# Two of five paired steps moved one place earlier, and three weight sums batched together

## The chip, the cores and the metric

The kernel runs on one core of one Trainium2 chip. The metric is the device time of one execution in microseconds. The program has one launch; its inputs are laid out on the host beforehand, by moving blocks only.

## The reference

One layer over 512 tokens of width 1024, in float32:

```python
h = rms_norm(x, norm_mix_g)
cb, cc, cin, q, k, v, f_logit, g_logit = jnp.split(h @ w_in, split_idx, axis=-1)
y_conv = (cb * causal_dwconv(cc * cin, conv_mix_w)) @ w_out_conv
y_attn = forgetting_attention(q, k, v, log_sigmoid(f_logit + b_f)) @ w_out_attn
g_conv, g_attn = jnp.split(sigmoid(g_logit + b_gate), 2, axis=-1)
x = x + (g_conv * y_conv + g_attn * y_attn) @ w_o
h = rms_norm(x, norm_ffn_g)
a, b = jnp.split(causal_dwconv(h @ w_up, conv_ffn_w), 2, axis=-1)   # 2 x 2816 wide
x = x + (silu(a) * b) @ w_down
return rms_norm(x, norm_f_g)
```

The change touches the last product pair: the up projection (1024 to 2 x 2816), its three-tap convolution along the sequence, and, by what it moves, the down projection.

## The kernel before

Activations lie transposed, channels on the 128 partitions and the 512 tokens along the free dimension. Every product is made of three float32r products: each operand is split into a high half (a copy, rounded) and a low half (the difference), and high x high, low x high and high x low are added in PSUM. For a weight tile the scalar engine makes the high half (`wh_...`, L279) and VectorE the low half (`wl_...`, L283) from what a DMA brought (`raw_...`, L221, issued by SyncE). There are five buffers for raw tiles and two each for the halves, so a split waits for TensorE to be done with the tile two before.

**Steps.** The hidden width is worked through in 22 steps `j` of 128 hidden channels, each with a tile of `a` and one of `b`. Steps 0 to 11 are the first half, then come 12 "down steps" that use what is there; steps 12 to 21 are the second half, followed by the remaining down steps and a plain remainder. A *plain* step is two blocks (`up{2j}`, `up{2j+1}`), each a full product over 8 blocks of the width, 48 matmuls of 128x256 (`p_up`). A block first runs 8 matmuls with the high half of the weight and then needs the low half. A *pair* (steps in `UPS`) multiplies its two tiles at once, as a two by two block product with seven instead of eight multiplications (Strassen's scheme in Winograd's form). Its weights come in four tiles, P, F, P, F (768, 1024, 768, 1024 columns), in which P holds plain blocks and F holds sums of blocks; its products (`us`) go to four PSUM banks and are combined by VectorE. Of each P the first 12 matmuls use the high half. The function `up_pair` does this, `pair` issues the products and asks for the splits.

**After the products** VectorE multiplies by the row scale (L1125, L1127: the evacuation, in place in PSUM for steps up to the last pair, and into the SBUF tile `xg` after it), `taps` makes the convolution (scalar engine L615, VectorE L616 and L619), and `glu` applies silu (L1147) and has GpSimd multiply (L1150 `ge` for an even step, L1157 `go` for an odd one). Two steps 2q and 2q+1 make one hidden pair `q`; with the odd one, `glu` puts off the sums of the hidden pair (L1167 to L1172) and their split into halves (scalar engine L1176, VectorE L1177, `gh`, `gl`). They are set free by the second, third and fourth weight split after that and stand between later splits. In the second half the taps and the `glu` of a pair are held back until the first block of the next step:

```python
z = p if j <= UPS[-1] else fz(f"fz{j}{s_}")
...
if j in UPS and ph:
    held_up.append(lambda: glu(ph, j, [tapped(j, s_, z) for s_, z in enumerate(uu)]))
```

With the last pair, once its products are done, the tile that held the summed inputs is used anew as `xg`: x1 is loaded into it (L1109, issued by GpSimd), and the scalar engine splits a part of it (L1358).

**Weight sums.** The F tiles are sums of weight blocks, which DMAs alone make in DRAM (`sum`): SyncE copies (L140) and GpSimd issues adding DMAs (L143), six operations for each group of two tiles, one at a time from a list (`tick`) as weights are split. `MIXED` says how many groups of the list take turns with each other: operation one of all of the batch, then operation two, and so on. Groups 14, 15 and 16 (`sum14` to `sum16`) belong to the three pairs of the second half, 17 to 19 to the down steps.

**Order.** On TensorE, GpSimd's DMAs and SyncE the order is that in which the program is written. On the scalar engine and VectorE a scheduler sets the order at build time, and each engine then runs its own in order. In the names of instructions a number after `up` is the tile (step 20 has `up40` and `up41`), and P36 to P41 are the P tiles of the three pairs.

Of the kernel before, what the change touches and what calls it, by code (L numbers as in the profile page):

```python
# [52 lines left out]
)  # L53
GS = 2
NFF = len(STEPS[0]) + len(STEPS[1])
UPS = (3, 7, 12, 15, 18)
NUP = NFF + 2 * (8 - GS)
MIXED = (4, 2, 4, 4, 2, 4, 2)

PLAIN = [(m, k) for m in (6, 7) for k in range(*PHASES[1])]  # L60
PCUTS = (0, 4, 12, 20)
# [3 lines left out]
def block_kernel(ctx, tc, xT, vecs, wv, win, wmix, wo, wup, wst, wdp, outT):  # L65
# [56 lines left out]
    for (j0, j1), n0, n1 in zip(PHASES, (0, len(STEPS[0])), (len(STEPS[0]), NFF - 1)):  # L122
        groups += [[NUP + 2 * i, NUP + 2 * i + 1] for i, j in enumerate(UPS) if j0 <= j < j1]
        groups += [list(range(n, min(n + 2, n1))) for n in range(n0, n1, 2)]
    groups.append([NFF - 1])
    nstep = [len(d) for d in STEPS[0] + STEPS[1]] + [2] * (2 * (KB - GS) + 2 * len(UPS))
    todo = []
# [26 lines left out]
    i0 = 0  # L154
    for n in MIXED:
        todo += [op for ops in zip(*map(group, range(i0, i0 + n))) for op in ops]
# [11 lines left out]
    def up_n(j):  # L168
        return [NUP + 2 * UPS.index(j) + d for d in range(2)]

# [14 lines left out]
    for ph, (j0, j1) in enumerate(PHASES):  # L185
        for j in range(j0, j1):
            if j in UPS:
                for m in up_n(j):
# [899 lines left out]
    def up_pair(j):  # L1088

        nonlocal xg, x1  # L1090
        flush([("xf", q) for q in range(4)])
        p23, p45, p16, p7 = banks = [acc(f"us{j}{i}") for i in range(4)]
        pair(up_n(j), x1_form, banks)
        z = fp.tile([P, S], F32, tag="fu", name=f"uz{j}", bufs=3)
        u = fp.tile([P, S], F32, tag="fu", name=f"uu{j}", bufs=3)[:, : S // 2]
        lo, hi = halves
        with after_split():
            nc.scalar.activation(z[:, lo], p16[:, lo], AF.Copy)
            nc.vector.tensor_add(z[:, hi], p16[:, hi], z[:, lo])
            nc.vector.tensor_add(u, p7[:, lo], z[:, hi])  # L1100
            nc.vector.tensor_add(z[:, hi], p45[:, hi], z[:, hi])
            nc.vector.tensor_add(p23, p23, z)
            p45h = p45.rearrange(halves_of, h=2)
            nc.vector.tensor_add(p45h, p45h, u.unsqueeze(1).to_broadcast([P, 2, S // 2]))
        if j == UPS[-1]:
            xg = xfp.tile([P, 4 * KB, 2 * P], F32, tag="xf", name="xg")
            x1 = xg[:, : 2 * KB].rearrange(whole, h=2)
            for a in range(0, KB, 4):
                nc.gpsimd.dma_start(x1[:, a : a + 4, :], x1d[:, a : a + 4, :])  # L1109
        return p23, p45  # L1110

    def up(ph, j, rb2, pu=None):
        uu = []
        if j in UPS:
            pu = up_pair(j)
# [416 lines left out]
```

## Time and profile before

| | |
|---|---|
| time, median of 3 runs | 690.75 us (690.72 to 690.81) |
| profiled execution | 690.7 us, span 688.9 us |
| granted TensorE clock, mean | 0.998 |
| TensorE busy | 680.0 us (99%) |
| VectorE busy | 547.3 us (79%) |
| scalar engine busy | 364.6 us (53%) |
| GpSimd busy | 184.2 us (27%) |
| second half's up steps, by TensorE's rows | 523.6 to 629.6 us |

A row of the timeline gives start, length, engine, line, operation, output<-inputs, and, in brackets, how long the engine had been idle and who ended that. Rows of one operation that follow each other are merged (x2). Matmuls overlap, so their pace is read from start to start, not from their lengths. PE is TensorE, DVE VectorE, ACT the scalar engine, POOL GpSimd, SPq the queue of SyncE.

### The profile page before, as it was taken

What the parts mean: (1) busy time and instruction counts of PE and PEld (TensorE: products, weight loads), DVE (VectorE), ACT (ScalarE), POOL (GpSimd) and SP (SyncE); (2) the same over time, 40 slices, a digit from 0 to 9 for tenths busy, and PEclk for the clock granted to TensorE, in tenths of its full rate; (3) what the DMA queues carried; (4) which work ended last, traced back from release to release, by engine and by line L of the source; (5) the groups of instructions that cost most, each with busy time, mean ns of one, the idle gap of its engine ahead of it and who ended that gap; (6) DMA issues with size and microseconds to landing.
All of it is one profiled execution on the core that took longest, in us unless ns stands there. A gap on an engine that the chain in (4) does not pass through costs nothing.

```text
span 688.9 us, 14690 instructions
## 1 busy us (share of the span) xinstructions
PE 680.0 (99%) x5916; PEld 677.8 (98%) x5916; DVE 547.3 (79%) x864; ACT 364.6 (53%) x581; POOL 184.2 (27%) x209
## 2 busy tenths in 40 slices
PE   9999999999999999999999999999999999999996
PEld 8999999999999999999999999999999999999996
DVE  6677777886687877768987989987665889999885
ACT  6575556554564544446654635545444445456563
POOL 5123745444021010233502141330131322222000
PEclk9999999999999999999999999999999999999999
DMA  8626957478579797888985859679799987674623
GB/s 295 208 89 217 198 154 174 100 184 167 131 221 279 214 262 197 240 270 281 213 225 133 227 119 293 156 216 253 219 290 309 251 193 183 187 239 132 188 78 123
DMA packets 66117, 139.64 MB, mean 203 GB/s; under 512 B 5856, under 2 KB 30432, under 8 KB 65792
## 3 DMA queue, kind: packets, MB, share of 16 engines
q1 hardware_dynamic: 44592, 105.72, 46.7%
q0 software_dynamic: 20736, 32.28, 26.9%
q8 instruction: 46, 0.75, 0.4%
q10 hardware_dynamic: 720, 0.69, 0.3%
q14 instruction: 23, 0.19, 0.1%
HBM read 132.32 MB, written 49.81 MB: 264 GB/s over the span
## 4 chain that ended last, share of the span: by engine, by line
PE 89%; DVE 6%; ACT 2%; issue 2%; DMA 1%; ACTq 0%; POOL 0%; SPq 0%; DVEq 0%; POOLq 0%
PE p_up L312 18%; PE p_in L312 14%; PE dn L330 13%; PE gs L330 8%; PE p_wo L312 6%; PE us L330 6%; PE p_up L330 6%; PE yc L330 3%; PE ya L312 3%; PE o L705 2%; PE pa L524 2%; PE pb L526 1%; PE tp L690 1%; PE pdB L312 1%; PE pdA L312 1%
## 5 line engine op out<-in xcount | busy, mean ns | idle before, releaser
L143 POOL DMA_DIRECT2D sum<-in_wst_dram x66 | 70.8, 1163 | 122.3 <-DMA sum<-sum 93.0
L312 PE MATMUL p_in<-xf,wh_in 128*128 128x256 f32 x576 | 95.7, 278 | 0.0
L312 PE MATMUL p_up<-x1h,wh_up 128*128 128x256 f32 x416 | 81.1, 276 | 0.0
L312 PEld LDWEIGHTS p_in<-xf,wh_in 128*128 128x128 f32 x576 | 80.4, 188 | 0.7
L312 PE MATMUL p_up<-x1l,wh_up 128*128 128x256 f32 x416 | 81.0, 276 | 0.0
L312 PE MATMUL p_up<-x1h,wl_up 128*128 128x256 f32 x416 | 80.9, 276 | 0.0
L279 ACT ACTIVATE wh_F<-raw_F 128x1024 fp32r<-128x1024 f32 (+1 forms) x42 | 44.2, 1052 | 66.7 <-PE dn L330 26.2
L283 DVE TENSOR_TENSOR wl_F<-raw_F,wh_F 128x1024 fp32r<-128x1024 f32 (+1 forms) x42 | 53.4, 1272 | 28.8 <-ACT wh_F L279 28.5
L312 PEld LDWEIGHTS p_up<-x1h,wh_up 128*128 128x128 f32 x416 | 62.7, 188 | 0.0
L312 PEld LDWEIGHTS p_up<-x1l,wh_up 128*128 128x128 f32 x416 | 62.6, 188 | 0.0
L312 PEld LDWEIGHTS p_up<-x1h,wl_up 128*128 128x128 f32 x416 | 62.5, 188 | 0.0
L312 PE MATMUL p_in<-xf,wl_in 128*128 128x256 f32 x288 | 56.6, 278 | 0.1
L279 ACT ACTIVATE wh_up<-raw_up 128x1024 fp32r<-128x1024 f32 x34 | 36.0, 1057 | 38.2 <-PE p_up L312 27.9
L279 ACT ACTIVATE wh_P<-raw_P 128x768 fp32r<-128x768 f32 (+1 forms) x42 | 35.1, 836 | 36.4 <-PE dn L330 15.9
L283 DVE TENSOR_TENSOR wl_P<-raw_P,wh_P 128x768 fp32r<-128x768 f32 (+1 forms) x42 | 40.2, 956 | 12.5 <-ACT wh_P L279 6.8
L283 DVE TENSOR_TENSOR wl_up<-raw_up,wh_up 128x1024 fp32r<-128x1024 f32 x34 | 42.3, 1246 | 7.6 <-ACT wh_up L279 7.6
L312 PEld LDWEIGHTS p_in<-xf,wl_in 128*128 128x128 f32 x288 | 43.5, 188 | 0.3 <-DVE wl_in L283 0.3
L1150 POOL TENSOR_TENSOR ge<-fu,fu 128x512 f32<-128x512 f32 x11 | 20.2, 1832 | 67.5 <-DVE fu L619 34.0
L330 PE MATMUL dn<-gh,wh_F 128*128 128x256 f32 x156 | 36.4, 276 | 0.0
L330 PE MATMUL dn<-gl,wh_F 128*128 128x256 f32 x156 | 36.3, 276 | 0.0
L283 DVE TENSOR_TENSOR wl_in<-raw_in,wh_in 128x1024 fp32r<-128x1024 f32 x24 | 30.2, 1258 | 6.1 <-ACT wh_in L279 6.0
L279 ACT ACTIVATE wh_in<-raw_in 128x1024 fp32r<-128x1024 f32 x24 | 25.3, 1056 | 10.8 <-issue 3.4
(361 smaller groups left out, 2106.0 us busy)
## 6 DMA issues: line engine op xcount, KB each, us to landing
raw_F<-sum SPq DMA_DIRECT2D x41, 512.0 KB, 5.4
raw_up<-in_wup_dram SPq DMA_DIRECT2D x34, 512.0 KB, 5.9
raw_P<-in_wst_dram SPq DMA_DIRECT2D x41, 384.0 KB, 4.8
raw_in<-in_win_dram SPq DMA_DIRECT2D x24, 512.0 KB, 3.6
sum<-in_wst_dram POOLq DMA_DIRECT2D x41, 256.0 KB, 6.3
sum<-in_wst_dram SPq DMA_DIRECT2D x20, 512.0 KB, 8.7
sum<-in_wst_dram POOLq DMA_DIRECT2D x20, 512.0 KB, 9.6
sum<-sum SPq DMA_DIRECT2D x40, 256.0 KB, 5.7
```

The costliest lines, as they stand in the source:

```text
L143: return lambda: keep(nc.gpsimd.dma_start(dst, src, accum_op=ALU.add))
L279: ins = nc.scalar.activation(hi, raw, AF.Copy)
L283: ins = nc.vector.tensor_sub(lo, raw, hi.bitcast(F32))
L312: keep(nc.tensor.matmul(out[:, cs], w, x[:, cs], start=start and i == 0 and c == 0, stop=stop and i == 2 and c == len(cut) - 1,))
L330: keep(nc.tensor.matmul(out, wl if x == 1 else wh, xl if x == 2 else xh, start=opens and bk not in seen, stop=closes and bk not in left,))
L524: keep(nc.tensor.matmul(pa[t][:, :VW], xt, w[:, :VW], start=start, stop=stop))
L526: keep(nc.tensor.matmul(pb[t], xt, w[:, VW:], start=start and t % 2 == 0, stop=stop and t % 2 == 1))
L690: keep(nc.tensor.transpose(tp[:, ks], pt[:, ks], ident))
L705: keep(nc.tensor.matmul(o[:, os_], vv[:, kb, pr, e, :], x[:, kb, cs], start=e == 0 and kb == 0 and i == 0, stop=e == 1 and kb == nk - 1 an ...
L1150: keep(nc.gpsimd.tensor_mul(ge, a.rearrange(halves_of, h=2), b.rearrange(halves_of, h=2)))
```

## The change

The second half's pairs are steps 12, 14 and 17 in place of 12, 15 and 18. The groups of weight sums stay the same in number; those of the three pairs now take turns in one batch of three, and those of the first three groups of down steps in another, in place of a batch of two and one of four. The last pair is one step earlier, and with it the load of x1 and the point from which evacuations go to `xg`.

```diff
-UPS = (3, 7, 12, 15, 18)
+UPS = (3, 7, 12, 14, 17)
 NUP = NFF + 2 * (8 - GS)
-MIXED = (4, 2, 4, 4, 2, 4, 2)
+MIXED = (4, 2, 4, 4, 3, 3, 2)
```

On VectorE, before, ahead of the first weight split of pair 18 (`go7`, `ge7`: sums of steps 14 and 15; `fu161`, `fu170`: taps of steps 16 and 17):

```order
L1167 TENSOR_TENSOR go7_7524<-ge7_7304 128x256
L619 SCALAR_TENSOR_TENSOR fu161_7581<-p_up33_7531,vec_64,fu161_7581 128x510
L1127 TENSOR_TENSOR p_up34_7588<-p_up34_7588,rb_n2_4660 128x512
L1168 TENSOR_TENSOR go7_7524<-go7_7524,ge7_7304 128x256
L1171 SCALAR_TENSOR_TENSOR go7_7524<-go7_7524 128x256
L1177 TENSOR_TENSOR gl_4720<-ge7_7304,gh_4719 128x2x256
L616 SCALAR_TENSOR_TENSOR fu170_7638<-p_up34_7588,vec_64,fu170_7638 128x511
L1172 SCALAR_TENSOR_TENSOR go7_7524<-go7_7524 128x256
L619 SCALAR_TENSOR_TENSOR fu170_7638<-p_up34_7588,vec_64,fu170_7638 128x510
L1177 TENSOR_TENSOR gl_4720<-go7_7524,gh_4719 128x512 x3
L283 TENSOR_TENSOR wl_P40_7725<-raw_P40_7420,wh_P40_7724 128x768
```

On the same engine in the changed program, ahead of the first weight split of step 20, two steps behind pair 17 (`go8`, `ge8`: sums of steps 16 and 17; `fu181`, `fu190`: taps of steps 18 and 19):

```order
L1167 TENSOR_TENSOR go8_7800<-ge8_7577 128x256
L619 SCALAR_TENSOR_TENSOR fu181_7857<-xg_7713,vec_64,fu181_7857 128x510
L1168 TENSOR_TENSOR go8_7800<-go8_7800,ge8_7577 128x256
L1127 TENSOR_TENSOR xg_7713<-p_up38_7864,rb_n2_4660 128x512
L1171 SCALAR_TENSOR_TENSOR go8_7800<-go8_7800 128x256
L1177 TENSOR_TENSOR gl_4720<-ge8_7577,gh_4719 128x2x256
L1172 SCALAR_TENSOR_TENSOR go8_7800<-go8_7800 128x256
L616 SCALAR_TENSOR_TENSOR fu190_7914<-xg_7713,vec_64,fu190_7914 128x511
L1177 TENSOR_TENSOR gl_4720<-go8_7800,gh_4719 128x512
L619 SCALAR_TENSOR_TENSOR fu190_7914<-xg_7713,vec_64,fu190_7914 128x510
L1177 TENSOR_TENSOR gl_4720<-go8_7800,gh_4719 128x512 x2
L283 TENSOR_TENSOR wl_up40_7999<-raw_up40_7693,wh_up40_7998 128x1024
```

The same operations stand ahead of a split in both; the split is now that of an up tile, the taps read `xg` in place of PSUM, and L1168 comes ahead of the evacuation.

On the scalar engine, before, behind the last pair (18), around the split of x1 (L1358):

```order
L615 ACTIVATE fu181_7933<-us181_7719,vec_64 128x512
L615 ACTIVATE fu190_7941<-xg_7852,vec_64 128x512
L1358 ACTIVATE gh_4719<-xg_7852 128x256
L279 ACTIVATE wh_up41_8060<-raw_up41_7801 128x1024
L1147 ACTIVATE fu180_7929<-fu180_7929 128x512
L615 ACTIVATE fu191_7995<-xg_7852,vec_64 128x512
```

And in the changed program, behind the last pair (17):

```order
L615 ACTIVATE fu171_7795<-us171_7580,vec_64 128x512
L615 ACTIVATE fu180_7803<-xg_7713,vec_64 128x512
L1358 ACTIVATE gh_4719<-xg_7713 128x256
L279 ACTIVATE wh_up39_7921<-raw_up39_7662 128x1024
L1147 ACTIVATE fu170_7791<-fu170_7791 128x512
L1176 ACTIVATE gh_4719<-ge8_7577 128x2x256
L1176 ACTIVATE gh_4719<-go8_7800 128x512
L615 ACTIVATE fu181_7857<-xg_7713,vec_64 128x512
```

L1358 with its load stands one step earlier, and behind it are now two splits of the hidden pair 16/17.

On GpSimd, before, near the end of the first half (`ge4`, `go4`, `ge5`: products of the hidden pairs 4 and 5; `sum14` to `sum16`: the pairs' weight sums):

```order
L1150 TENSOR_TENSOR ge4_5786<-fu80_5720,fu81_5781 128x512
L143 DMA sum14_98<-in_wst_dram 256x1x256
L143 DMA sum15_99<-in_wst_dram 256x1x256
L1157 TENSOR_TENSOR go4_5924<-fu90_5850,fu91_5915 128x512
L143 DMA sum14_98<-in_wst_dram 256x1x256
L1150 TENSOR_TENSOR ge5_6054<-fu100_5984,fu101_6049 128x512
```

And in the changed program:

```order
L1150 TENSOR_TENSOR ge4_5786<-fu80_5720,fu81_5781 128x512
L143 DMA sum16_100<-in_wst_dram 256x1x512
L1157 TENSOR_TENSOR go4_5924<-fu90_5850,fu91_5915 128x512
L143 DMA sum14_98<-in_wst_dram 256x1x256
L143 DMA sum15_99<-in_wst_dram 256x1x256
L1150 TENSOR_TENSOR ge5_6054<-fu100_5984,fu101_6049 128x512
```

The third pair's first add now stands in the first half, and the second adds of the first two are one product later.

## The prediction

> **What bounds the kernel now.** I read the page first, then who TensorE waited for, then its rows around the one wait that lies in the changed stretch.
>
> ```profile
> PE 680.0 (99%) x5916; PEld 677.8 (98%) x5916; DVE 547.3 (79%) x864; ACT 364.6 (53%) x581; POOL 184.2 (27%) x209
> ...
> PE warm L108 <- DVE ones L100: 1.1, 1, 1.1
> PE us L330 <- DVE wl_P L283: 0.9, 1, 0.9
> ```
>
> TensorE is busy for 99% of the span, and of the waits listed for it only one is in the second half: products of a pair, waiting for the low half of a weight that VectorE splits (`wl_P`). Here it is in TensorE's own rows (start, length, engine, line, operation, count):
>
> ```profile
> 564.42 0.28 PE L330 MATMUL p_up<-x1h,wh_up 128*128 128x256 f32 x1
> ...
> 575.30 0.28 PE L330 MATMUL p_up<-x1h,wh_up 128*128 128x256 f32 x1
> ...
> 586.18 0.28 PE L330 MATMUL us<-x1h,wh_P 128*128 128x256 f32 x1
> ...
> 588.65 0.50 PE L330 MATMUL us<-x1h,wl_P 128*128 128x256 f32 x2 [0.94 <-DVE wl_P L283]
> ...
> 596.93 0.28 PE L330 MATMUL p_up<-x1h,wh_up 128*128 128x256 f32 x1
> ```
>
> From 564.42 (pair 15 done, step 16 begins) to 575.30 are 96 matmuls: 0.1133 us each. So a block of 48 takes 5.44 us, a plain step 10.88, a pair (84) 9.52. Pair 18 runs from 586.18 to 596.93, 10.75 us: **1.23 us are lost there**. Its first 12 matmuls need only the high half (1.36 us, up to 587.54); the 13th came at 588.65, 1.11 late, and 0.12 more goes in restarting. This 1.23 is all that the change can win in this stretch, 0.18% of the run.
>
> Why the split was late stands in VectorE's rows, with GpSimd's one beside them:
>
> ```profile
> 579.86 0.75 DVE L616 SCALAR_TENSOR_TENSOR fu<-p_up,vec,fu 128x511 f32<-128x511 f32 x1 [0.26 <-ACT fu L615]
> ...
> 581.52 0.69 DVE L1127 TENSOR_TENSOR p_up<-p_up,rb_n 128x512 f32<-128x512 f32 x1
> 582.11 1.22 DVE L1168 TENSOR_TENSOR go<-go,ge 128x256 f32<-128x256 f32 x1
> 583.25 0.42 DVE L1171 SCALAR_TENSOR_TENSOR go<-go 128x256 f32<-128x256 f32 x1
> ...
> 585.84 1.88 DVE L1177 TENSOR_TENSOR gl<-go,gh 128x512 fp32r<-128x512 f32 x3
> 587.64 0.95 DVE L283 TENSOR_TENSOR wl_P<-raw_P,wh_P 128x768 fp32r<-128x768 f32 x1
> ...
> 581.75 1.30 POOL L1150 TENSOR_TENSOR ge<-fu,fu 128x512 f32<-128x512 f32 x1 [3.23 <-DVE fu L619]
> ```
>
> VectorE works through a pile: the evacuation of pair 15, its taps (held back into step 16), and then the sums and the splits of the hidden pair 14/15 (L1167 to L1177), which an odd step sets off and an even one does not. The pile is through two steps after the odd pair, and the split stands behind it.
>
> **The change part by part.** TensorE's rows are the same number in both programs, so the same 5916 matmuls run; only their order moves, at 0 us. What counts is where VectorE's pile meets TensorE.
>
> *Pair 15 becomes 14.* An even pair sets off no sums, so the pile of 15 is gone; steps 15 and 16 carry the splits of 12/13 and the taps of 14, and the sums of 14/15 come at the end of pair 17, as those of 12/13 came at the end of pair 15, where nobody waited. I take the wait at a pair's `wl_P` as gone: **-1.23 us**.
>
> Pair 14 begins one step after pair 12 and its first products go into the bank that holds pair 12's first sum until the taps have read it:
>
> ```profile
> 542.33 1.40 DVE L619 SCALAR_TENSOR_TENSOR fu<-us,vec,fu 128x510 f32<-128x510 f32 x2
> ...
> 544.02 0.28 PE L330 MATMUL p_up<-x1h,wh_up 128*128 128x256 f32 x1
> ```
>
> Step 14 starts at 544.02, and the first of the two tap rows is done near 543.0: 1.0 us of cover, and a little more afterwards, since the split ahead of it is that of a P, 0.95 by the row above, and no longer that of a wider up weight. Costed at 0; if the taps came 2 us late, 1 us would show.
>
> *Pair 18 becomes 17.* This is the term that decides. Pair 17 is odd, so it has a pile of its own, which in the changed order stands ahead of `wl_up` of step 20, two plain steps on, just as pair 15's stood ahead of `wl_P` of pair 18. Call T the end of the pair. Three things differ.
>
> First, an up block needs its low half sooner: after 8 matmuls, 0.91 us, instead of 12. The need is at T + 21.76 + 0.91 = T + 22.67 (before: T + 23.12).
>
> Second, the last pair is also the point after which evacuations go to SBUF (`xg`), and where x1 is loaded. In the old program this came with the even pair 18, and its rows are the model, T being 596.93:
>
> ```profile
> 597.40 1.17 POOL L1109 DMA_DIRECT2D xg<-x1d  x2 [0.83 <-PE us L330]
> 608.03 0.42 ACT L1358 ACTIVATE gh<-xg 128x256 fp32r<-128x256 f32 x1 [1.59 <-DMA xg<-x1d]
> ...
> 610.00 1.78 POOL L1150 TENSOR_TENSOR ge<-fu,fu 128x512 f32<-128x512 f32 x1
> ...
> 610.12 2.22 DVE L619 SCALAR_TENSOR_TENSOR fu<-xg,vec,fu 128x510 f32<-128x510 f32 x1
> 612.25 1.21 DVE L283 TENSOR_TENSOR wl_up<-raw_up,wh_up 128x1024 fp32r<-128x1024 f32 x1
> 613.39 0.74 DVE L616 SCALAR_TENSOR_TENSOR fu<-xg,vec,fu 128x511 f32<-128x511 f32 x1
> ...
> 577.22 1.30 POOL L1157 TENSOR_TENSOR go<-fu,fu 128x512 f32<-128x512 f32 x1 [5.08 <-DVE fu L616]
> ...
> 577.60 0.75 DVE L619 SCALAR_TENSOR_TENSOR fu<-p_up,vec,fu 128x510 f32<-128x510 f32 x1
> ```
>
> A tap that reads `xg` while GpSimd multiplies took 2.22 us; the same tap out of PSUM (`p_up`), also under a GpSimd product, 0.75. VectorE's order behind pair 17 is, row by row, that behind the old pair 18 up to the L616 at 613.39, which is T + 16.46. Behind pair 15 this place was at 579.86 - 564.42 = T + 15.44. So 1.02 us later.
>
> [...]
>
> Third, from there to the split. In the old rows 579.86 to 587.64 is 7.78 us, of which the L1168 row, caught by the product at 581.75, has 1.22 - 0.42 = 0.80 too much: 6.98 bare. The new order holds the same operations, but L1168 stands ahead of the evacuation, and the evacuation, out of PSUM, ran freely beside a product in these rows:
>
> ```profile
> 615.05 0.68 DVE L1127 TENSOR_TENSOR xg<-p_up,rb_n 128x512 f32<-128x512 f32 x1
> ...
> 615.30 1.29 POOL L1157 TENSOR_TENSOR go<-fu,fu 128x512 f32<-128x512 f32 x1 [3.52 <-DVE fu L619]
> ...
> 615.65 2.02 DVE L283 TENSOR_TENSOR wl_up<-raw_up,wh_up 128x1024 fp32r<-128x1024 f32 x1
> ...
> 596.31 0.42 DVE L1168 TENSOR_TENSOR go<-go,ge 128x256 f32<-128x256 f32 x1
> 596.64 0.42 DVE L1171 SCALAR_TENSOR_TENSOR go<-go 128x256 f32<-128x256 f32 x1
> ```
>
> So I let L1168 (0.33 from start to start, 596.31 to 596.64) and the evacuation (0.60) pass before L1171 is caught, for what is left of 1.3 and its start-up: 0.55. The bounds are 0 and 1.3. Sum: 16.46 + 6.98 + 0.55 + 1.21 (the split, by the 612.25 row) + 0.06 (from its end at 588.59 to TensorE's 588.65) = T + 25.26. Against the need at T + 22.67 TensorE waits 2.59, with the restart 2.71: **+2.71 us**. As a check, the same sum for the old place is 15.44 + 7.78 + 0.95 + 0.06 = 24.23, minus 23.12 = 1.11, as measured.
>
> Queued behind that split on VectorE are an evacuation and the next `wl_up`, which TensorE needs 5.44 us later; VectorE is through both about 2 us after the first. `wl_up` of step 19's second block ends at T + 16.53 (612.25 + 1.21), needed at T + 17.23: 0.7 of cover. If x1 lands later, L1358 holds up the scalar engine, and the product, the tap and L616 behind it move by as much less 0.3; I allow 1 us above.
>
> *One batch of three.* The three pair sums take turns, so the copies and adds of the third run in the first half, and adds move past products in GpSimd's queue:
>
> ```profile
> 438.28 3.08 POOL L1150 TENSOR_TENSOR ge<-fu,fu 128x512 f32<-128x512 f32 x1 [2.75 <-ACT gh L1176]
> ...
> 448.37 0.48 SPq L221 DMA_DIRECT2D raw_F<-sum  x1
> ...
> raw_F<-sum SPq DMA_DIRECT2D x4, 512.0 KB, 6.5
> ...
> sum<-in_wst_dram POOLq DMA_DIRECT2D x3, 512.0 KB, 10.2
> ...
> 466.50 0.28 PE L330 MATMUL dn<-gh,wh_P 128*128 128x256 f32 x1
> ```
>
> The third's first add now stands behind the product that ends at 441.4; with about 1 us to issue and 10.2 to landing (the last number of the DMA rows) it is there near 452, and SyncE's second copy waits for it, ahead of the first F load of the down steps. That load goes out near 452.5 instead of 448.4. TensorE comes to the down steps at 466.5, so 7 us of cover are left after a transfer of 6.5: 0. If that cover were gone, each us late would cost a us. The adds of the last three groups queue behind no product that TensorE waits for.
>
> **Sum.** -1.23 + 2.71 = +1.48 us. On the profiled execution (690.7 us, span 688.9) that is 692.2; the median of the runs, 690.75, is the same number for this purpose. [...]
>
> **The rivals.**
>
> *A: the pile passes free of GpSimd* (not slower). If the products fall beside operations that they don't block, L616 is at T + 15.44 and nothing is caught behind it: 15.44 + 6.98 + 1.21 + 0.06 = 23.69, a wait of 1.02, 1.14 with the restart: net -0.1, 690.6 us. It turns on whether the product of pair 17 starts before the L619 of step 18 begins or after it has ended. For it: product and tap need meet only by chance. Against: both hang on the same scalar row (L1358), so they met in the model. 0.2.
>
> *B: no new wait*, the old one gone: 690.7 - 1.23 = 689.5. For that VectorE would have to be 1.0 us faster still than in A, and no row shows where. 0.07.
>
> *C: x1 is late or both products catch the chain*: +1.2 on the forecast, 693.4. For it: x1 took 10.6 us to land and shares the queues with weight sums. 0.13. TensorE's clock belongs here (in the last two rows: length, busy time, granted clock, DMA):
>
> ```profile
> 682.07 0.61 PE L392 MATMUL pb_n<-ident,rc_n 128*128 128x128 f32 x4
> ...
> 685.00:686.00 1.00, 0.00 (x0) 1.00 1.10 385
> 686.00:687.00 1.00, 0.00 (x0) 0.82 1.09 384
> ```
>
> After its last matmul, done at 682.7, the granted clock stayed at 1.00 into the slice from 686: about 4 us. A wait of 2.6, and C's 3.8, keep it. [...]
>
> *D: the batch of three starves the down steps*: a wait of 2 to 4 us near 466, where the rows leave 7 us: 694. 0.05.
>
> **How the numbers follow.** The forecast, +1.5 with 0.6 to 2.4 as its own range, has 0.55. A measurement of this kernel can tell 0.2%, 1.4 us, from no change, and the forecast lies nearly on that line: I give it 0.33 slower and 0.22 same. C and D add 0.18 to slower, A 0.2 to same, B (0.18% faster) 0.03 to faster and 0.04 to same. Slower 0.51, same 0.46, faster 0.03. The range is 690.0 to 693.5: A and C are in, B and D out.
>
> **What would show it.** In the profile after: no wait of `us` for `wl_P`; one wait of `p_up` at L330 for `wl_up` of 2 to 3 us near 607; ahead of it in VectorE's rows three L1177, and further ahead an L619 on `xg` of about 2 us beside a GpSimd product. A wait near 466, or one at pair 14 near 544, would show the parts wrong that I put at 0; a wait under 1.2 us near 607 is A.

## The result and the profile after

The changed kernel takes **698.48 us** (median of four runs, 697.15 to 700.26), the kernel before 690.78 in the same set: a ratio of **1.0113**, 95% interval 1.009 to 1.0136. It is slower by 7.7 us; the forecast was 692.2, with a range of 690.0 to 693.5. A second set of runs of the same kernel, further down, gave 697.53.

The profiled execution took 697.15 us (span 695.4) against 690.7 (span 688.9): 6.5 us of span. Its page, with the busy times and two rows of the 40 slices (tenths of TensorE's busy time and of its granted clock):

```profile
PE 682.3 (98%) x5916; PEld 680.3 (98%) x5916; DVE 546.9 (79%) x864; ACT 364.1 (52%) x581; POOL 181.1 (26%) x209
...
PE   9999999999999999999999999999999999979996
...
PEclk9999999999999999999999999999999999989999
```

One slice, the 36th (608 to 626 us), holds the loss: TensorE is busy for less of it, and its clock is lower. The two longest entries in the list of TensorE's waits (tile that waited, releaser, us in total, times, longest) say for whom:

```profile
PE p_up L330 <- DVE wl_up L283: 5.0, 1, 5.0
PE warm L108 <- DVE ones L100: 1.1, 1, 1.1
```

The old wait of `us` for `wl_P` is gone, and there is one new wait, at the forecast place and for the forecast tile. It is 5.0 us long and not 2.6. TensorE's rows from the end of pair 17 (584.83, the time T) through step 20:

```profile
584.83 0.28 PE L330 MATMUL p_up<-x1h,wh_up 128*128 128x256 f32 x1
...
606.59 0.28 PE L330 MATMUL p_up<-x1h,wh_up 128*128 128x256 f32 x1
...
607.38 0.28 PE L330 MATMUL p_up<-x1l,wh_up 128*128 128x256 f32 x1
612.71 1.22 PE L330 MATMUL p_up<-x1h,wl_up 128*128 128x256 f32 x4 [5.05 <-DVE wl_up L283]
...
615.86 0.63 PE L312 MATMUL p_up<-x1l,wh_up 128*128 128x256 f32 x2
...
618.63 0.39 PE L312 MATMUL p_up<-x1h,wh_up 128*128 128x256 f32 x2
...
619.31 0.28 PE L330 MATMUL p_up<-x1h,wh_up 128*128 128x256 f32 x1
```

Step 20 begins at 606.59 = T + 21.76, as worked out. Its first block runs until 619.31, 12.72 us in place of 5.44: **7.28 us are lost**. Of these 5.22 are the late 9th matmul, the first that needs the low half (612.71 in place of 607.38 + 0.11 = 607.49). The other 2.06 come after it: a row of two matmuls is 0.63 long at 615.86 and 0.39 at 618.63. The stretches of that time show why (length, busy time of PE, PEld, DVE, ACT and POOL, granted clock, DMA):

```profile
606.50:610.00 3.50, 1.16 (x11) 0.96 (x9) 3.50 (x7) 1.98 (x3) 1.43 (x2) 1.00 0.29 37
610.00:613.50 3.50, 0.80 (x3) 0.80 (x4) 3.50 (x6) 1.73 (x3) 0.00 (x0) 0.51 0.13 38
613.50:616.75 3.25, 3.25 (x17) 3.25 (x17) 2.88 (x5) 0.57 (x1) 0.56 (x1) 0.50 0.49 161
617.00:618.00 1.00, 1.00 (x11) 1.00 (x10) 0.45 (x2) 0.00 (x0) 1.00 (x2) 1.00 0.00 0
```

The granted clock went to 0.50 near 610.0, in the middle of the wait, and came back near 617. Some 0.1 of the 2.06 is the restart, an estimate by the 0.12 of the old wait. So the balance is -1.23 (the old wait) + 5.22 (the new one) + 2.06 (the clock and the restart) = +6.05. TensorE's last group of matmuls starts exactly that much later than before, at 688.12 against 682.07; the other 0.4 us of the span lie behind it.

Where the wait comes from stands in the rows of the scalar engine, GpSimd and VectorE behind pair 17:

```profile
585.30 1.16 POOL L1109 DMA_DIRECT2D xg<-x1d  x2 [1.76 <-PE us L330]
...
600.45 1.75 POOL L1157 TENSOR_TENSOR go<-fu,fu 128x512 f32<-128x512 f32 x1 [6.38 <-ACT fu L1147]
...
598.43 0.42 ACT L1358 ACTIVATE gh<-xg 128x256 fp32r<-128x256 f32 x1 [4.10 <-DMA xg<-x1d]
...
602.23 0.63 ACT L1176 ACTIVATE gh<-go 128x512 fp32r<-128x512 f32 x1 [1.40 <-POOL go L1157]
602.77 0.71 ACT L615 ACTIVATE fu<-xg,vec 128x512 f32<-128x512 f32 x1
...
598.01 0.74 DVE L619 SCALAR_TENSOR_TENSOR fu<-xg,vec,fu 128x510 f32<-128x510 f32 x1
...
603.93 0.75 DVE L616 SCALAR_TENSOR_TENSOR fu<-xg,vec,fu 128x511 f32<-128x511 f32 x1 [2.88 <-ACT fu L615]
...
606.54 0.91 DVE L1171 SCALAR_TENSOR_TENSOR go<-go 128x256 f32<-128x256 f32 x1
...
611.44 1.21 DVE L283 TENSOR_TENSOR wl_up<-raw_up,wh_up 128x1024 fp32r<-128x1024 f32 x1
```

The load of x1 left at T + 0.47, as before, but landed 13.1 us later (585.30 to 598.43) and not 10.6. The scalar engine stood idle for 4.10 us on it, with L1358 at the head of its queue; behind L1358 it had the L615 that VectorE's L616 needs, and VectorE stood idle for 2.88. From L616 to the split it then took 611.44 - 603.93 = 7.51 us, against 6.98 + 0.55 = 7.53 in the forecast.

### The profile page after: what moved, and what is told of

Read it like the earlier page. It is cut to its first block, busy times and chain, and to the rows that moved or that the text cites. A ratio compares the mean times of both kernels' runs of the same rounds, so it can differ in the third digit from the quotient of the medians.

```text
span 695.4 us, 14696 instructions
## 1 busy us (share of the span) xinstructions
PE 682.3 (98%) x5916; PEld 680.3 (98%) x5916; DVE 546.9 (79%) x864; ACT 364.1 (52%) x581; POOL 181.1 (26%) x209
## 4 chain that ended last, share of the span: by engine, by line
PE 90%; DVE 5%; ACT 2%; issue 1%; DMA 0%; POOL 0%; ACTq 0%; SPq 0%; DVEq 0%; POOLq 0%
PE p_up L312 18%; PE p_in L312 14%; PE dn L330 13%; PE gs L330 8%; PE us L330 6%; PE p_wo L312 6%; PE p_up L330 5%; PE yc L330 3%; PE ya L312 3%; PE pa L524 2%; PE pb L526 2%; PE p_g L312 2%; PE o L705 2%; PE tp L690 1%; PE pdB L312 1%
## 5 line engine op out<-in xcount | busy, mean ns | idle before, releaser
L1150 POOL TENSOR_TENSOR ge<-fu,fu 128x512 f32<-128x512 f32 x11 | 17.4, 1585 | 84.4 <-DVE fu L619 44.0
L330 PE MATMUL dn<-gl,wh_F 128*128 128x256 f32 x156 | 36.3, 276 | 0.0
L330 PE MATMUL dn<-gh,wh_F 128*128 128x256 f32 x156 | 36.3, 276 | 0.0
```

What stands on the lines that cost most here:

```text
L330: keep(nc.tensor.matmul(out, wl if x == 1 else wh, xl if x == 2 else xh, start=opens and bk not in seen, stop=closes and bk not in left,))
L1150: keep(nc.gpsimd.tensor_mul(ge, a.rearrange(halves_of, h=2), b.rearrange(halves_of, h=2)))
```

## The experiments

**The parts of the change.** The edits that are to be compared are single numbers of the table of pairs and of the batches.

*Pair 14 and the batch, the last pair left at 18:*

```
-UPS = (3, 7, 12, 14, 17)
+UPS = (3, 7, 12, 14, 18)
```

> Pairs 12, 14 and 18, with the new batches of weight sums: half of the change, pair 15 to 14; the last pair stays at 18, an even step. Theory 1 and theory 2 alike: no sums stand ahead of pair 18's first split, nor ahead of step 20's behind an even last pair, so the old wait of 1.23 us goes and none comes: 689.5 us. A third theory (the batch of three in itself, or pair 14 right behind pair 12, costs time): more than 691.5.

Measured: 689.35 us (688.49 to 689.86, ten runs), ratio to before 0.9976 [0.9967, 0.9985]. TensorE's list of waits has one line:

```profile
PE warm L108 <- DVE ones L100: 1.1, 1, 1.1
```

The old wait at pair 18 is gone and none took its place: the -1.23 of the forecast is real (-1.44 in the medians). This version is faster than both kernels, than the one before by 0.24%.

*Pair 17, with the other one left at 15:*

```
-UPS = (3, 7, 12, 14, 17)
+UPS = (3, 7, 12, 15, 17)
```

> Pairs 12, 15 and 17, with the new batches: the other half, pair 18 to 17. Theory 1 and 2: the order ahead of step 20's split is that of the changed kernel, so its wait and its halved clock are there: 697 to 700 us, with the spread of the changed kernel's runs. If the loss came from pair 14 or from both moves together, it would be below 692.

Measured: 696.84 us (695.28 to 696.97), ratio 1.0081 [1.0064, 1.0097], with a wait of 4.0 us for `wl_up` of step 20 and the clock at 0.50 there. The loss comes with pair 17. Its rows of x1:

```profile
588.14 1.44 POOL L1109 DMA_DIRECT2D xg<-x1d  x2
...
597.87 0.42 ACT L1358 ACTIVATE gh<-xg 128x256 fp32r<-128x256 f32 x1 [3.23 <-DMA xg<-x1d]
```

Here x1 was late in another way: it took only 9.73 us, but GpSimd issued it 3.00 us after the end of the pair (585.14), behind an adding DMA of the weight sums that had waited 2.94 us for another. So the scalar engine waited for x1 in both programs, and the reason in the changed one is asked further down.

*The old batches with the new pairs.* With them the third pair's weights are read before their sums are finished, so that this part computes on unfinished sums.

```
-MIXED = (4, 2, 4, 4, 3, 3, 2)
+MIXED = (4, 2, 4, 4, 2, 4, 2)
```

> Pairs 12, 14 and 17, with the old batches of weight sums (two and four): VectorE's order is that of the changed kernel. Theory 1 with the load of x1 slow because of the weight sums that are issued just ahead of it: x1 lands within about 10.6 us and the time falls to 692 to 694. Theory 1 with the load slow whatever runs beside it, or theory 2: 697 to 700. If the third pair's sums, now in a batch with the down steps', come late for pair 17, a new wait of TensorE at its F weights near 576 us, some us more.

Measured: 696.14 us (695.87 to 696.34), ratio 1.0077 [1.0062, 1.0092]; x1 again took 13.1 us (585.24 to 598.36) and the wait was 5.0 us. The batch of three does not make x1 late in the changed kernel. (Its profiled execution, 696.34 us, is 0.8 below that of the changed kernel; no wait in the two lists tells them apart.)

*The new batches with the old pairs:*

```
 UPS = (3, 7, 12, 15, 18)
-MIXED = (4, 2, 4, 4, 2, 4, 2)
+MIXED = (4, 2, 4, 4, 3, 3, 2)
```

> The kernel before (pairs at steps 15 and 18) with the new batches of weight sums alone (three pairs' sums in one batch). If the batch is worth nothing, as it was costed, the time is within 0.2% of 690.8 us: 690.0 to 691.5, and no new wait of TensorE over 0.5 us. If the larger batch starves the down steps (case D of the forecast), TensorE waits for weights in the down steps and the time is 693 us or more.

Measured: 690.71 us (690.35 to 692.44), ratio 0.9999 [0.999, 1.0008]. The wait of the kernel before is there, of the same length, and no new one, so the batch costs nothing:

```profile
PE us L330 <- DVE wl_P L283: 0.9, 1, 0.9
```

**Is it x1 at the head of the scalar engine's queue?** The split of x1 (L1358 and the subtraction behind it) is moved into the down steps, where its result is used; the loads stay where they are.

```
 (in the down steps)
+            if ph and n == 2:
+                y7 = x1[:, KB - 1, halves[1]]
+                with after_split():
+                    nc.scalar.activation(gh[:, 41, :], y7, AF.Copy)
+                    nc.vector.tensor_sub(gl[:, 41, :], y7, gh.bitcast(F32)[:, 41, :])
 (behind the last pair)
-    y7 = x1[:, KB - 1, halves[1]]
-    nc.scalar.activation(xlast[0], y7, AF.Copy)
-    nc.vector.tensor_sub(xlast[1], y7, xlast[0].bitcast(F32))
```

> The changed kernel, with the scalar engine's and VectorE's split of x1 (L1358, L1359) moved from step 18 into the third of the last down steps. Nothing else moves on VectorE ahead of the weight split of step 20. Theory 1 (x1's load lands about 13 us after its issue and, through L1358, holds up the scalar engine, then the product of pair 17, the tap of step 18 and the pile): the tap L616 is at about T + 16 in place of T + 19.1 (T: end of pair 17), TensorE's wait before step 20 falls from 5.2 us to 1.9 to 2.6, and the run to 691.5 to 692.5 if the granted clock holds, up to 694 if it halves again. Theory 2 (the pile alone makes the wait): the wait stays near 5 us and the time near 698.

Measured: 692.5 us (691.91 to 693.73, ten runs), ratio 1.0027 [1.0017, 1.0036]. Its list of waits has, in the second half:

```profile
PE p_up L330 <- DVE wl_up L283: 1.8, 1, 1.8
```

Two rows of VectorE:

```profile
598.07 1.45 DVE L619 SCALAR_TENSOR_TENSOR fu<-xg,vec,fu 128x510 f32<-128x510 f32 x1
...
600.71 0.75 DVE L616 SCALAR_TENSOR_TENSOR fu<-xg,vec,fu 128x511 f32<-128x511 f32 x1
```

L616 comes at 600.71 and not at 603.93, the wait is 1.8 us, the clock stays at 1.00, and 6.0 of the 7.7 us are gone (5.0 of 6.5 by the second set of runs of the changed kernel). So the wait of 5 us with its slow clock needs x1 at the head of the queue; that the 1.8 us left are VectorE's pile is asked next.

**Is the rest the pile?** In the changed kernel the GLU of an odd step calls `flush()`, which issues whatever was still put off of the hidden pair before (its sums and splits, not the weight sums in DRAM), so that the pile stands ahead of the next split. Here one split is called ahead of it:

```
+            if ph and j - 2 in UPS and len(parts) == chunk.n:
+                split()
```

> The changed kernel with one more split asked for ahead of the sums that an odd step flushes out, so that on VectorE the low half of step 20's first weight stands ahead of the pile (L1167 to L1177) and no longer behind it. x1's split still holds up the scalar engine. If the wait is made of the pile (6.2 of 7.5 us behind the tap L616 at T + 19.1) on top of the late x1: the low half is done at about T + 22.5, TensorE needs it at T + 22.67, the wait is 0 to 0.5 us, the clock holds, and the run takes 689.5 to 690.2 us. If the late x1 alone makes the wait, it stays above 2 us and the time above 692.

Measured: 692.43 us (691.57 to 694.32, ten runs), ratio 1.0019 [1.0008, 1.0029]. The wait was cut to two pieces with 1.8 us in all, the longer one now at the next split, behind the pile:

```profile
PE p_up L330 <- DVE wl_up L283: 1.8, 2, 1.4
```

The profiled execution is the slowest of its ten runs (x1 took 13.8 us in it), so its rows are not compared further. This edit alone takes off as much as the one before it: neither cause is the larger, since either one alone leaves a wait of 1.8 us at the full clock. Both edits together, x1 split late and one split ahead of the pile:

> The changed kernel with both: x1's split in the last down steps, and step 20's split ahead of the pile. Both theories: no wait of TensorE near step 20, 689.5 us (the old 690.7 less 1.23), and runs that differ by less than those of the changed kernel.

Measured: 690.43 us (689.67 to 692.38, ten runs), ratio 0.9991 [0.9982, 1.0001]. No wait of the second half is left in the list. The two causes together are all of the wait; in time it is 0.9 us short of the expectation, and this 0.9 has no wait of TensorE to its name.

The same extra split in the kernel before asks whether the old wait had the same cause:

> The kernel before (pairs at steps 15 and 18) with one weight split called ahead of the GLU of the odd step two after a pair, so that pair 18's first wl_P stands ahead of the weight sums that the GLU of step 17 flushes. If that pile is the cause of the old wait of 1.2 us for wl_P, the wait goes and the time is about 690.8 - 1.2 = 689.6 us. If the next split only waits in its place, behind the pile, the time stays at 690.3 to 691.

Measured: 690.0 us (689.62 to 691.58, eleven runs), ratio 0.9987 [0.9978, 0.9995], and the wait for `wl_P` is gone from the list. The old wait was the pile behind an odd pair, by the edit and not only by the rows.

**Why does x1 land later?** Both kernels' DMA views from the issue of x1 to its landing, the change's first (585.2 to 598.5), then that of before (597.3 to 608.1; queue, packets, MB, share; below, KB each and median us to landing):

```profile
q1 hardware_dynamic: 710, 1.94, 38.7%
...
raw_up<-in_wup_dram SPq DMA_DIRECT2D x2, 512.0 KB
```

```profile
q1 hardware_dynamic: 459, 0.80, 19.2%
...
raw_up<-in_wup_dram SPq DMA_DIRECT2D x1, 512.0 KB
```

In the changed kernel two weight loads of 512 KB leave on SyncE's queue around the issue of x1. The row at 584.73 merges them: the first leaves at 584.73, 0.57 us ahead of x1, the second at 586.58, 1.28 us behind it:

```profile
582.94 1.68 SPq L140 DMA_DIRECT2D sum<-in_wst_dram  x2
584.73 2.19 SPq L221 DMA_DIRECT2D raw_up<-in_wup_dram  x2
600.24 1.35 SPq L140 DMA_DIRECT2D sum<-sum  x2
```

In the kernel before, the last two weight loads had left at 591.88 and 593.82, 5.5 and 3.6 us ahead of x1. Then the order of SyncE's queue had copies of sums that wait, and the next weight load left at 602.75, 5.4 us after x1's issue. A first trial to get the needed half of x1 sooner changed the order of x1's two loads:

```
-            for a in range(0, KB, 4):
+            for a in (4, 0):
```

> The changed kernel with the two loads of x1 in the other order: the half that the scalar engine's split L1358 reads is asked for first. VectorE's order is the same. If x1's landing sets the wait (theory 1) and the first of two loads lands sooner than the last (13.1 us), L1358 comes some us sooner, the tap L616 with it, TensorE's wait falls below 3.5 us and the time to 692 to 695. If the landing sets nothing, 696 to 700 as before. If both loads move together through the queues, the landing and the time stay.

Measured: 698.51 us (697.65 to 698.95), ratio 1.0105 [1.0089, 1.012]. The half that L1358 needs did land sooner, after 9.85 us, but the scheduler had put L1358 one split further ahead in the scalar engine's queue:

```profile
595.17 0.42 ACT L1358 ACTIVATE gh<-xg 128x256 fp32r<-128x256 f32 x1 [8.66 <-DMA xg<-x1d]
...
605.18 0.73 PE L330 MATMUL p_up<-x1h,wl_up 128*128 128x256 f32 x4 [1.52 <-DVE wl_up L283]
...
613.94 1.23 PE L330 MATMUL p_up<-x1h,wl_up 128*128 128x256 f32 x4 [2.96 <-DVE wl_up L283]
```

The engine idled 8.66 us on it, and TensorE waited three times for the splits behind it (0.69, 1.52 and 2.96 us). The trial changed two things at once and says nothing on the loads; it says that where L1358 stands matters as much as when x1 lands. The second trial holds the two weight loads back:

```
             if held[0] == NRAW:
                 return
+            if nm == "up41" and len(parts) < [x for x, *_ in stream].index("up39"):
+                return
```

> The changed kernel, with the two 512 KB weight loads that SyncE issues at 584.73 us, just ahead of the load of x1, held back until the split two ahead of the one that waits: they then stand behind the copies of the weight sums on SyncE's queue and go out at about 600 us. If these two loads are what makes the load of x1 take 13.1 us, it lands in 10 to 11 us as before, L616 of step 18 comes about 2.5 us earlier, TensorE waits about 2.6 us for wl_up of step 20, the clock stays at 1.00, and the time is 692 to 694 us. If it is the sums on GpSimd's own queue (two accumulating loads of 256 KB issued at 581.40, which stand ahead of x1), x1 still takes 12.5 us or more, the wait is still 4.5 us or more, and the time is 696.5 to 699 us.

Measured: 695.62 us (695.51 to 696.32), ratio 1.0069 [1.0056, 1.0083], between the two expectations. The rows of GpSimd, the scalar engine, VectorE and TensorE (lines are two higher in this kernel):

```profile
585.33 1.16 POOL L1111 DMA_DIRECT2D xg<-x1d  x2 [1.77 <-PE us L332]
...
598.21 2.86 POOL L1159 TENSOR_TENSOR go<-fu,fu 128x512 f32<-128x512 f32 x1 [4.10 <-DVE xg L1129]
...
596.19 0.42 ACT L1360 ACTIVATE gh<-xg 128x256 fp32r<-128x256 f32 x1 [1.83 <-DMA xg<-x1d]
...
602.80 0.75 DVE L618 SCALAR_TENSOR_TENSOR fu<-xg,vec,fu 128x511 f32<-128x511 f32 x1 [2.89 <-ACT fu L617]
...
611.57 0.74 PE L332 MATMUL p_up<-x1h,wl_up 128*128 128x256 f32 x4 [3.88 <-DVE wl_up L285]
```

x1 lands after 10.86 us, 2.27 sooner, with the sums on GpSimd's queue where they were (581.42): the two loads are what made it late. The wait falls only by 1.2, to 4.0, since half of the gain is given back one step later. The product `go`, which follows x1's split, now begins while VectorE is on a tap and a split, takes 2.86 us in place of 1.75, and the scalar engine has to wait for it before its L615 (L617 here).

**What the slow clock costs.** In the wait, 36 matmuls on data that is there anyway, into a bank that nobody reads:

```
+            if fill and n == 8:
+                to = bank(6, "keep")
+                for i in range(36):
+                    keep(nc.tensor.matmul(to[:, : 2 * P], fill[0][:, :P], fill[1][:, 0, : 2 * P], start=True, stop=True))
...
-                    ], 4)
+                    ], 4, (wh, xh) if name == "up40" else None)
```

> The changed kernel with 36 more matmuls (128x256, into a bank that nobody reads, 4.1 us at full pace) put into TensorE's wait of 5.2 us ahead of step 20's low half. They add work that counts for nothing, in time in which TensorE stood still. If the wait costs its length and no more: the same time, 697 to 700. If it also halves the granted clock for what comes after it (2.1 us in the profile of the changed kernel): no row below 1.00 there, and 2 us less, 695 to 698.

Measured: 695.82 us (695.33 to 696.0), ratio 1.0066 [1.0051, 1.0081]: 2.7 us less than the changed kernel in the medians.

```profile
606.69 0.28 PE L334 MATMUL p_up<-x1h,wh_up 128*128 128x256 f32 x1
...
607.60 4.24 PE L332 MATMUL keep<-x1h,wh_up 128*128 128x256 f32 x36
612.47 0.73 PE L334 MATMUL p_up<-x1h,wl_up 128*128 128x256 f32 x4 [0.63 <-DVE wl_up L283]
...
617.20 0.28 PE L334 MATMUL p_up<-x1h,wh_up 128*128 128x256 f32 x1
```

The wait for the split is filled, the clock stays at 1.00, and the block takes 617.20 - 606.69 = 10.51 us in place of 12.72, 2.21 less. Of these 0.35 are a split that came a little sooner (the first matmul that needs it is 612.47 - 607.60 = 4.87 late and not 5.22); the other 1.86 are the clock's. Against the second set of runs of the changed kernel the medians differ by 1.7 and not 2.7.

**The changed kernel once more.**

> The changed kernel once more, unchanged, for a second profile and a second set of times. If the loss is the wait of 5.2 us plus the slow clock, the profile again shows x1 landing 12.5 to 13.5 us after its issue, one wait of 4.8 to 5.4 us for wl_up of step 20, and the granted clock at 0.50 for a whole number of stretches of 3.41 us, one, two or three, by where the clock's window stands. By two such stretches the time is 696.5 to 697.5, as in the first profile; the median of 698.5 of the first set then has something that the first profile doesn't show. If the window's place varies from run to run, the times spread over 2 us or more again.

Measured: 697.53 us (696.44 to 697.69), ratio 1.0089 [1.0071, 1.0107]. In the profile x1 landed after 13.0 us, the wait was 4.9, and the clock was low from 611.06 to 617.89, 6.83 us, twice the 3.41 us of the run with the loads held back. The block took 619.77 - 606.70 = 13.07 us, so that 5.10 were the wait (612.70 against 607.60) and 2.53 the clock and the restart, half a microsecond more than in the first profile. The median of 698.48 and the highest run of 700.26 of the first set lie above what either profile accounts for (697.15 and 697.50); what these runs had beside is open.

## Why the prediction was wrong, point by point

- **The old wait, -1.23 us.** Right. It went with pair 14 alone (0.9976), and it went in the kernel before by one split ahead of the pile (0.9987).
- **Place and tile of the new wait, and that it outweighs the old one.** Right: one wait, `p_up` at L330 for `wl_up`, step 20, need at T + 22.67 (607.49 - 584.83 = 22.66 measured).
- **From L616 to the split, 7.53 us.** Right, 7.51. L1171 took 0.91 us at 606.54, beside a GpSimd product (605.83 to 607.17), against 0.42 bare in the kernel before, so 0.49 where 0.55 was put. The product `go`, too, took 2.86 us beside VectorE's tap and split with the loads held back, where it took 1.75 in the changed kernel. Why these rows are longer was not shown.
- **L616 at T + 16.46.** This is the first step that failed: it came at T + 19.10, 2.64 later. The term was "x1 lands as before", with 1 us allowed above. It landed in 13.1 us and not 10.6, +2.50, and L1358 to L616 took 5.50 and not 5.36, +0.14. I had compared the order on VectorE, the scalar engine and GpSimd behind the last pair, and not what SyncE issues around x1.
- **The way to L616 was wrong even where its sum was right.** I had taken the tap L619 on `xg` as caught (2.22 us) and the queue of VectorE as the limit. In fact L619 took 0.74, VectorE was idle for 2.88, and L616 waited for the scalar engine, whose L615 stands behind the split of `go` and so behind a GpSimd product. That 5.50 is near 5.36 is chance: with x1 in time (the two loads held back, T = 584.86) the same stretch took 602.80 - 596.19 = 6.61. So the forecast's number would not have come out with x1 on time either: L616 was then at T + 17.94 and the wait 4.0.
- **"Waits of 2.6 and 3.8 keep the clock."** The second step that failed, worth 2.06 us with the restart in the first profile and 2.53 in the second. One row on one idle stretch was read as a fixed delay of 4 us. The clock fell 2.4 us after the last matmul had ended here.
- **Rival C** (x1 late) was the case, with 0.13; its mechanism was right, its price of 1.2 us should have been 2.6 and the clock besides. (With the forecast's own bounds, x1 1 us later and 1.3 in place of 0.55, its sum comes to +3.2, 693.9, which its range up to 693.5 left out; the measured time is far beyond both.) Rival A's condition held for the tap: the product began at 600.45, after L619 had ended at 598.75. Its time did not follow, since L616 then waited for the scalar engine, and behind it L1171 was caught. B is out: the wait was there. D is out: 0.9999 for the batch alone.
- **Pair 14's start and the batch of three, both at 0.** Right: no wait near 544 or 466 in the profile after.

## What to carry to other kernels

When a step that issues a load is moved, look at what the other DMA queues issue around it in the new order, too: two weight loads that had left 3.6 us or more ahead of x1 now left within 1.3 us of it, and made it 2.3 us later. An operation that waits for a load, put on the scalar engine ahead of work that others need, hands the load's lateness on to them: 2.50 us in the landing became 2.64 in L616. Splitting x1 where it is used took 6.0 of the 7.7 us away, and so did one weight split called ahead of the pile. And a wait of TensorE has to be priced with the clock: the waits of 2.96 us and more lowered it here, the one of 1.77 us did not, and with the restart it added 2.06 and 2.53 us to waits of 5.05 and 4.93.

## What the runs showed of the clock

The low clock comes in stretches of one length. The bounds can be read from slices of 0.25 us, since the slices show 1.00 or 0.50 everywhere but at the bounds: in the changed kernel,

```profile
610.00:610.25 0.25, 0.00 (x0) 0.00 (x0) 0.25 (x2) 0.00 (x0) 0.00 (x0) 0.62 0.04 4
...
616.75:617.00 0.25, 0.25 (x3) 0.25 (x3) 0.00 (x0) 0.00 (x0) 0.25 (x1) 0.73 0.00 0
```

it fell at 610.06 (0.62 is 0.19 us of low clock in the slice) and rose at 616.88 (0.73: 0.13 us more), 6.82 us. With the two loads held back it was

```profile
612.50:612.75 0.25, 0.25 (x4) 0.25 (x3) 0.25 (x1) 0.25 (x1) 0.00 (x0) 0.53 0.15 49
...
615.75:616.00 0.25, 0.25 (x3) 0.25 (x3) 0.00 (x0) 0.00 (x0) 0.25 (x1) 0.64 0.00 0
```

from 612.52 to 615.93, 3.41 us. The other runs with such a wait gave 6.83 (pair 17 alone), 6.83 (old batches), 3.41 (x1's loads swapped) and 6.83 (the second profile of the change): one or two times 3.41. With the loads held back the clock fell 0.95 us after TensorE had gone on working at 611.57. By these runs the fall goes by how much of a stretch of 3.41 us with fixed bounds was idle, and not by how long ago the last matmul was. That the bounds are fixed shows at the kernel's end, where the clock falls once more: in the changed kernel at 691.98, 75.10 us after the rise at 616.88, which is 22 stretches of 3.414. With pair 17 alone, with the old batches and with x1's loads swapped it is 75.1 us there, too (by slices of 5 us), though in these four runs the last matmul had ended 4.2, 3.2, 2.6 and, in the changed kernel, 3.3 us before that fall. Counting back 3.41 us from each fall: 2.25 us idle with the old batches (last matmul ended at 607.61, fall at 609.86), 2.40 in the changed kernel (607.66 to 610.06), 2.46 with the loads held back (609.11 to 611.57) and 2.38 with the loads swapped (613.94 - 2.96 = 610.98 to 613.36) were enough. The wait of 1.77 us without x1 at the head of the queue was not, though it lay in one stretch (607.72 to 609.49; 22 stretches back from the fall at that kernel's end, at 684.9 by slices of 5 us, the bounds are 606.4 and 609.8). These figures are from waits between matmuls 256 columns wide. At the end of that same kernel, where the fall came 1.3 us after the last matmul (683.58), idle time alone does not account for it; what else counts there was not shown. The 4.0 us at the kernel's end, which the forecast took as a fixed delay, fit as well: the fall at 686.65 ends a stretch that began at 683.24 and was all idle, and in the one before it only 683.24 - 682.68 = 0.56 us were idle.

So the fall is not a fixed delay after the last matmul: in the two profiles of the changed kernel alone it came 2.4 and 3.3 us after it. Had the wait been the forecast's 2.6 us, it would, by an estimate from the 2.25 us that were enough and the 1.77 that were not, have cost the clock only where a stretch happened to stand around it; that was not tried.
